# Early gathered rows taken out of their own phase and set among the scattered columns

## The chip, the cores and the metric

The kernel runs on one core of a Trainium2 chip. The metric is the device time of one execution in microseconds (us): the median of 3 runs of the kernel before is 1791.42 us (1790.85 to 1795.96). The profiled execution took 1794.13 us, of which the profile's span covers 1792.4 us. Engines are named as the profile names them: PE (matmul), PEld (its weight load), DVE (vector), ACT (scalar), POOL (GpSimd), SP (the queue that issues most DMAs).

## The reference

One decoder layer: an S5 branch and an mLSTM branch, merged by gates, and then a PEER expert mixer. Only the mixer is touched. For each of 512 tokens and 8 heads it finds the 16 best of 128 x 128 experts and adds up their value rows, weighted by a softmax gate and the expert's activation:

```python
q = (xb @ w_q).reshape(BLOCK, PEER_HEADS, 2, PEER_HALF)
s = jnp.einsum('thid,hikd->thik', q, keys32)
sv, si = lax.top_k(s, PEER_TOPK)                 # per half-key
cs, ci = lax.top_k(cand, PEER_TOPK)              # of the 16 x 16 sums
eidx = jnp.take_along_axis(cidx, ci, axis=-1)
gate = jax.nn.softmax(cs, axis=-1)
act = jax.nn.gelu(jnp.einsum('td,thkd->thk', xb, u_tab[eidx]))
return jnp.einsum('thk,thkd->td', gate * act, v_tab[eidx])
```

## The kernel before, in words

The 512 tokens are four tiles of 128. Tiles 1 to 3 are computed densely: for each of 128 blocks j of 128 experts, a hidden tile `h` = u_j x (the tokens of tiles 1 to 3) is made on PE in 24 matmuls of 128x384 (eight k steps of three matmuls, since each operand is split into a high and a low part: ACT makes `uh`, DVE makes `ul`), ACT applies the GELU (`act`), the result is multiplied by the dense gate (`w`), and products with v_j are added up in PSUM (`o`). Tile 0 is computed by gathering instead: for each of its 128 choices per token, POOL fetches one row per token of the table u (`fetch`, an indirect DMA of 512 KB) and DVE multiplies it with the tokens and adds up (`use`); later the same with rows of v.

The dense gates come by two ways. Tiles 2 and 3: `gates(i, ...)`, in 16 steps each of four one-hot instructions on DVE, 16 small matmuls on PE (`gp`), two evictions on ACT (`stg`), and a 2 MB store to DRAM (`gd`) after every fourth step. Tile 1: `scatter(n)`, which adds one column (one choice of each of the 128 tokens) into a zeroed array in DRAM (`gds`) by an indirect DMA with addition, issued by POOL. Columns of one head go beside each other; the first column of a head waits until all 16 columns of the head before have landed. Each is also put behind the last low split `wql` (`lows`), which POOL makes for the score blocks. The product phase reads `gds` only when the last head has landed.

What leads up to it: 16 score blocks (`scores(s_)`: the projection with w_q, the scores, the first top 16 on DVE); then `pairs_of` finds the 16 best pairs, per tile (tile 1 in two halves of four heads; the first half is traced in the middle of the score blocks, after block 8). The first half of tile 1's index list is `ix` (line 1170). `e0` (line 1293) is tile 0's index list, from which the gathers read.

The order of the work. `fill(us)` is called after each piece of that work with the piece's weight in us. It adds the weight to `done[0]`, issues two columns if columns have begun, and traces quarters of hidden tiles (two k steps) of the list `todo`, so that their count (280 quarters, 70 tiles) keeps step with `done[0]` over `whole` (236 us). Ten more tiles (`LEFT`) are traced behind all of that. The score loop issues two columns after each of the blocks 13 to 15 (line 1285). After the gates of tiles 2 and 3, `scatter(P)` issues what columns remain, and then `early()` asks for the first 40 (`NEARLY`) rows of u for tile 0, with four buffers, each used two fetches later, with `fill(1.3)` between. The buffers (`vraw`) are later those of the rows of v.

The trace order isn't yet the order on the engines: a planner orders the instructions of each engine ahead of the run, by trace order and by its own account of when operands are ready. `keep_in_program_order(i)` puts an instruction behind the instruction of the same engine that was traced just before it (it may be later, not earlier). On the chip each engine then takes its instructions in that fixed order. In the kernel before, the early gathers and their uses are pinned in this way and the columns are not.

Of the kernel before, what the change touches and what calls it, by code (L numbers as in the profile page):

```python
# [11 lines left out]
F32 = mybir.dt.float32  # L12
F32R = mybir.dt.float32r
BF16 = mybir.dt.bfloat16
# [9 lines left out]
P = 128  # L24
D = 1024
# [900 lines left out]
def peer(tc, a, out, dbg, cst, dram, xh, xl, blanks, ident, h2d, gds, x0, qt01, dump, split, mm3, rsqrt_cols):  # L926
# [21 lines left out]
    with es:  # L948
# [4 lines left out]
        ad = dram.tile([len(SP_), P, SD], F32, name="ad")  # L953
        acts = {}

        def load(j, eng):

            raw = up.tile([P, NK, P], F32, tag="uraw", name=f"u{j}", bufs=3)
            SY.dma_start(raw, a["ut"][j])
            hi = up.tile([P, NK, P], F32R, tag="uhi", name=f"uh{j}", bufs=3)  # L960
            lo = up.tile([P, NK, P], F32R, tag="ulo", name=f"ul{j}", bufs=3)
            split(hi, lo, raw, eng)
            return hi, lo

        def hidden(j, k0=0, k1=NK, eng=V):

            if k0 == 0:
                acts[j] = *load(j, eng), hps.tile([P, SD], F32, tag="h", name=f"h{j}")
            hi, lo, p = acts[j]
            for k in range(k0, k1):  # L970
                mm3(p, hi[:, k], lo[:, k], xh[k // 4][:, k % 4, P:], xl[k // 4][:, k % 4, P:], k == 0, k == NK - 1)
            if k1 == NK:
                acts[j] = up.tile([P, SD], F32, tag="act", name=f"act{j}", bufs=RA + 3)
                A.activation(acts[j], p, AF.Gelu_apprx_tanh)  # L974
                if j in SP_:
                    SY.dma_start(ad[SP_.index(j)], acts.pop(j))
# [13 lines left out]
        def fetch(s_, t):  # L990

            rows[s_], c = t, s_ % P
            return GP.indirect_dma_start(out=t, out_offset=None, in_=a["u"] if s_ < P else a["v"],  # L993
                                         in_offset=bass.IndirectOffsetOnAxis(ap=e0[:, c:c + 1], axis=0))

        def use(s_, jk):

            g, c = rows.pop(s_), s_ % P
            if s_ < P:
                i_ = V.scalar_tensor_tensor(jk, g, 1.0, x0, op0=OP.mult, op1=OP.mult, accum_out=hsl[:, c:c + 1])  # L1000
                if s_ == P - 1:
                    A.activation(hsl, hsl, AF.Gelu_apprx_tanh)
                    tt(w0, w0, hsl, OP.mult)
            elif c == 0:
                i_ = V.tensor_scalar(ac0, g, w0[:, 0:1], None, op0=OP.mult)
            else:
                i_ = V.scalar_tensor_tensor(ac0, g, w0[:, c:c + 1], ac0, op0=OP.mult, op1=OP.add)  # L1007
            return i_

        def early():  # L1010

            jk = rw.tile([P, D], BF16, name="jke", bufs=1)
            for n in range(NEARLY + 2):
                if n < NEARLY:
                    tc.keep_in_program_order(fetch(n, up.tile([P, D], F32, tag="vraw", name=f"ge{n}", bufs=4)))
                if n >= 2:
                    tc.keep_in_program_order(use(n - 2, jk))
                yield

        rp = ExitStack()  # L1020
        rm = rp.enter_context(tc.tile_pool(name="rm", bufs=1, reuse_waits="tile"))
# [151 lines left out]

        cols = []

        def scatter(n):

            for ix, wt, c in cols[:n]:
                i_ = GP.indirect_dma_start(out=gds.rearrange("b i j t -> (b i j t)").unsqueeze(1),  # L1179
                                           out_offset=bass.IndirectOffsetOnAxis(ap=ix[:, c:c + 1], axis=0),  # L1180
                                           in_=wt[:, c:c + 1], in_offset=None, compute_op=OP.add)

                h = c // TOPK
                if c % TOPK == 0:
                    heads.append([])
                for o in heads[h]:
                    tc.declare_no_dep(i_.ins, o.ins, reason="columns of one head")
                for o in heads[h - 1] if h else blanks:
                    behind(i_, o)
                heads[h].append(i_)  # L1190
                behind(i_, lows[-1])
            del cols[:n]

        heads = []
# [3 lines left out]
            tc.add_manual_dep(ins.ins, on.ins.name, mybir.DependencyInfo(  # L1198
                mybir.DependencyClass.Sync, mybir.DependencyReason.DATA), reason="gates added up")

        def gates(i, beside):

            ef, w = prs[i][1].rearrange("p h k -> p (h k)"), prs[i][2]
            p = mp.tile([P, 2, P], F32, tag="tr", name=f"et{i}")
            PE.transpose(p[:, 0], ef, ident)
            PE.transpose(p[:, 1], w, ident)
            ei = rw.tile([P, 2, P], I32, tag="ei", name=f"ei{i}", bufs=1)
            V.tensor_copy(ei[:, 0], p[:, 0])
            V.tensor_scalar(ei[:, 1], ei[:, 0], NKEY - 1, None, op0=OP.bitwise_and)
            V.tensor_scalar(ei[:, 0], ei[:, 0], 7, None, op0=OP.logical_shift_right)  # L1210
            eb = rw.tile([P, 2, P], F16, tag="eb", name=f"eb{i}", bufs=1)
            V.tensor_copy(eb, ei)

            wt = rw.tile([P, 2, P], F32, tag="wt", name=f"wt{i}", bufs=1)
            wb = rw.tile([P, 2, P], F16, tag="wb", name=f"wb{i}", bufs=1)
            V.tensor_scalar(wt[:, 0], p[:, 1], GS, None, op0=OP.mult)
            V.tensor_copy(wb[:, 0], wt[:, 0])
            tt(wt[:, 1], wt[:, 0], wb[:, 0], OP.subtract)
            V.tensor_copy(wb[:, 1], wt[:, 1])

            sh = [P, 4, P, 2]
            io_ = iob.unsqueeze(1).to_broadcast(sh)

            def each(x):
                return x.rearrange("p (a t) -> p a t", t=2).unsqueeze(2).to_broadcast(sh)
            for b in range(P // TB):
                stg = rw.tile([P, NKEY, TB], F32, tag="stg", name=f"stg{i}{b}")
                for q in range(TB // 8):
                    c = slice(b * TB + q * 8, b * TB + q * 8 + 8)
                    o1 = rw.tile(sh, F16, tag="o1", name=f"o1{i}{b}{q}")  # L1230
                    o2 = rw.tile(sh, F16, tag="o2", name=f"o2{i}{b}{q}")
                    ow = rw.tile([P, 2] + sh[1:], F16, tag="ow", name=f"ow{i}{b}{q}")
                    tt(o1, io_, each(eb[:, 0, c]), OP.is_equal)
                    tt(o2, io_, each(eb[:, 1, c]), OP.is_equal)
                    for n in range(2):
                        tt(ow[:, n], o2, each(wb[:, n, c]), OP.mult)
                    for h in range(2):
                        p = mp.tile([P, 4, P], F32, tag=("mm", "sc", "tr")[(2 * q + h) % 3], name=f"gp{i}{b}{q}{h}")
                        for t in range(4):
                            for n in range(2):  # L1240
                                a_, b_ = 2 * h + t // 2, t % 2
                                PE.matmul(p[:, t], o1[:, a_, :, b_], ow[:, n, a_, :, b_], start=n == 0, stop=n == 1)
                        t0 = 8 * q + 4 * h
                        A.activation(stg[:, :, t0:t0 + 4].rearrange("p j t -> p t j"), p, AF.Copy, scale=1.0 / GS)
                    fill(2.7)
                    for _ in range(2):
                        next(beside, None)
                SY.dma_start(gd[(i - 2) * (P // TB) + b], stg)

        def ready(j):  # L1250
# [6 lines left out]
        todo = [(j, h) for j in SP_[:-LEFT] for h in range(4)]  # L1257
        ntodo = len(todo)
        done = [0.0]

        whole = 4 * 24 + 2 * 16 * 2.75 + NEARLY * 1.3

        def fill(us):

            done[0] += us
            if heads:
                scatter(2)
            while todo and (ntodo - len(todo)) * whole < done[0] * ntodo:
                j, h = todo.pop(0)
                hidden(j, 2 * h, 2 * h + 2)  # L1270
# [6 lines left out]
        def beside_gates():  # L1277
            yield from filled(3)

        for s_ in range(NSEG):  # L1280
            scores(s_)
            if s_ == NSEG // 2:
                for _ in filled(1, 0, PH // 2):
                    pass
            if s_ > NSEG - 4:
                scatter(2)
        rq.close()
        rw = rp.enter_context(tc.tile_pool(name="rw", bufs=2, reuse_waits="tile"))
        for of in ((1, PH // 2, PH), (0,), (2,)):
            for _ in filled(*of):  # L1290
                pass
            if of == (0,):
                V.tensor_copy(e0, prs[0][1].rearrange("p h k -> p (h k)"))
        rest = beside_gates()
        for i in (2, 3):
            gates(i, rest)
        scatter(P)
        for _ in early():
            fill(1.3)
        for j, h in todo + [(j, h) for j in SP_[-LEFT:] for h in range(4)]:  # L1300
            hidden(j, 2 * h, 2 * h + 2)
        for j in range(RA):
            ready(j)
        rp.close()
# [150 lines left out]
```

## Time and profile before

| what | value |
|---|---|
| median of 3 runs | 1791.42 us (1790.85 to 1795.96) |
| profiled execution: time, span | 1794.13 us, 1792.4 us |
| PE busy | 1696.9 us (95% of the span) |
| DVE busy | 1314.6 us (73%) |
| ACT busy | 709.5 us (40%) |
| POOL busy | 728.7 us (41%) |
| mean granted TensorE clock | 0.978 |
| DMA | 412.11 MB, mean 230 GB/s |

How to read it: busy shares are means over the span, and stages differ. A wait is put down to what released it. A busy PE isn't PE at its peak, and spans on POOL are rough. A granted clock of 1.0 is 2.4 GHz, 0.5 is 1.2 GHz. In the timelines a row is: start in us, duration in us, engine, line, operation, output<-inputs, count, and in brackets the engine's idle time before it with what ended that. In tables of groups: busy us, mean ns of one | idle us before, with the releasers.

### The profile page before, as it was taken

The page shows a single profiled execution, that of the slowest core. Times are in us where ns is not written, and L with a number is a line of the kernel's source. Part 1 is how long each engine was busy: PE and PEld are TensorE (multiplying, and loading weights), DVE is VectorE, ACT ScalarE, POOL GpSimd, SP SyncE. Part 2 cuts the span into 40 slices and gives each one's busy share as a digit, 9 for nine tenths or more (in the row PEclk, how much of TensorE's full clock was granted, in tenths as well). Part 3 has the DMA queues.
Part 4 walks back from the last instruction along what each step waited for, and adds up shares of the span by engine and source line. Part 5 has one row for each costly group of instructions (what it writes and reads, how often), then busy time and mean ns, then how long its engine had stood idle before and what let it go on. Part 6 is the DMA issues. An engine that isn't in the chain of part 4 may idle for free. (4 is left out here: it accounts for less than half of the span.)

```text
span 1792.4 us, 25268 instructions
## 1 busy us (share of the span) xinstructions
PE 1696.9 (95%) x9196; PEld 1489.1 (83%) x9196; DVE 1314.6 (73%) x2584; ACT 709.5 (40%) x1064; POOL 728.7 (41%) x500
## 2 busy tenths in 40 slices
PE   5998989999999999999966999999999999999997
PEld 5988767776787889999956998888888888888885
DVE  7984583334657979996926668888878888888887
ACT  4533615443332324466732334333333333333333
POOL 2002433221313267787775433343333334444450
PEclk9989989999999999999987999999999999999999
DMA  4543325211343326768858999999899999999994
GB/s 164 126 77 91 105 95 176 71 48 36 120 178 137 113 52 167 178 201 258 245 159 310 360 378 383 348 328 376 326 356 327 363 324 363 323 363 322 334 340 177
DMA packets 206357, 412.11 MB, mean 230 GB/s; under 512 B 49176, under 2 KB 122904, under 8 KB 205080
## 3 DMA queue, kind: packets, MB, share of 16 engines
q1 hardware_dynamic: 142288, 267.49, 43.9%
q0 software_dynamic: 55296, 134.31, 22.6%
q10 hardware_dynamic: 8648, 8.70, 1.7%
q8 instruction: 72, 1.18, 0.3%
q14 instruction: 53, 0.43, 0.1%
HBM read 360.00 MB, written 47.28 MB: 227 GB/s over the span
## 5 line engine op out<-in xcount | busy, mean ns | idle before, releaser
L87 PE MATMUL h<-x2h,ul 128*128 128x384 f32 x1024 | 345.0, 337 | 31.0 <-DVE ul L80 31.0
L83 PE MATMUL h<-x2h,uh 128*128 128x384 f32 x1024 | 346.5, 338 | 3.0 <-ACT act L974 3.0
L86 PE MATMUL h<-x2l,uh 128*128 128x384 f32 x1024 | 344.7, 337 | 0.0
L86 PE MATMUL o<-vl,wh 128*128 128x512 f32 x768 | 299.7, 390 | 1.7 <-DVE vl L80 1.7
L87 PE MATMUL o<-vh,wl 128*128 128x512 f32 x768 | 295.3, 390 | 0.0
L83 PE MATMUL o<-vh,wh 128*128 128x512 f32 x768 | 286.8, 391 | 2.9 <-ACT wh L79 2.9
L993 POOL DMA_INDIRECT g<-in_v,e x128 | 168.6, 1317 | 238.0 <-DVE ac L1007 76.8
L1179 POOL DMA_INDIRECT gds<-gw,ix x128 | 235.4, 1839 | 61.1 <-issue 36.5
L87 PEld LDWEIGHTS h<-x2h,ul 128*128 128x128 f32 x1024 | 193.4, 189 | 33.3 <-DVE ul L80 31.3
L80 DVE TENSOR_TENSOR ul<-u,uh 128x1024 fp32r<-128x1024 f32 x128 | 156.1, 1220 | 87.6 <-ACT uh L79 82.9
L79 ACT ACTIVATE uh<-u 128x1024 fp32r<-128x1024 f32 x128 | 135.6, 1061 | 180.6 <-PE h L86 151.2
L83 PEld LDWEIGHTS h<-x2h,uh 128*128 128x128 f32 x1024 | 193.5, 189 | 5.8 <-ACT act L974 3.4
L86 PEld LDWEIGHTS h<-x2l,uh 128*128 128x128 f32 x1024 | 193.5, 189 | 2.5
L79 ACT ACTIVATE wh<-w 128x384 fp32r<-128x384 f32 x128 | 66.7, 524 | 296.8 <-issue 159.4
L993 POOL DMA_INDIRECT g<-in_u,e x88 | 111.8, 1271 | 175.7 <-DVE jk L1000 91.6
L80 DVE TENSOR_TENSOR vl<-v,vh 128x1024 fp32r<-128x1024 f32 x128 | 156.2, 1221 | 30.2 <-ACT vh L79 28.9
L83 PEld LDWEIGHTS o<-vh,wh 128*128 128x128 f32 x768 | 143.9, 188 | 33.1 <-ACT wh L79 4.9
L86 PEld LDWEIGHTS o<-vl,wh 128*128 128x128 f32 x768 | 144.2, 188 | 31.0 <-DVE vl L80 2.2
L87 PEld LDWEIGHTS o<-vh,wl 128*128 128x128 f32 x768 | 144.2, 188 | 29.0
L1007 DVE SCALAR_TENSOR_TENSOR ac<-g,w,ac 128x1024 f32<-128x1024 f32 x127 | 162.5, 1279 | 0.3
L79 ACT ACTIVATE vh<-v 128x1024 fp32r<-128x1024 f32 x128 | 134.0, 1049 | 62.8 <-PE o L87 56.8
L80 DVE TENSOR_TENSOR wl<-w,wh 128x384 fp32r<-128x384 f32 x128 | 70.5, 556 | 53.3 <-ACT wh L79 53.0
(540 smaller groups left out, 3170.8 us busy)
## 6 DMA issues: line engine op xcount, KB each, us to landing
u<-in_ut SPq DMA_DIRECT2D x128, 512.0 KB
v<-in_v SPq DMA_DIRECT2D x128, 512.0 KB
gd<-stg SPq DMA_DIRECT2D x8, 2048.0 KB
gi<-gd SPq DMA_DIRECT2D x32, 512.0 KB
ad<-act SPq DMA_DIRECT2D x80, 192.0 KB
acl<-ad SPq DMA_DIRECT2D x80, 192.0 KB
gds<-qt SPq DMA_DIRECT2D x8, 1024.0 KB
gi<-gds SPq DMA_DIRECT2D x32, 256.0 KB
```

Source lines behind the costliest of these rows:

```text
L79: A.activation(hi, src, AF.Copy)
L80: return eng.tensor_tensor(lo, src, f32(hi), op=OP.subtract)
L83: i_ = PE.matmul(ps, lh, rh, start=first, stop=False)
L86: PE.matmul(ps, lh, rl, start=False, stop=False)
L87: return PE.matmul(ps, ll, rh, start=False, stop=last)
L993: return GP.indirect_dma_start(out=t, out_offset=None, in_=a["u"] if s_ < P else a["v"], in_offset=bass.IndirectOffsetOnAxis(ap=e0[:, c:c ...
L1007: i_ = V.scalar_tensor_tensor(ac0, g, w0[:, c:c + 1], ac0, op0=OP.mult, op1=OP.add)
L1179: i_ = GP.indirect_dma_start(out=gds.rearrange("b i j t -> (b i j t)").unsqueeze(1), out_offset=bass.IndirectOffsetOnAxis(ap=ix[:, c:c + 1 ...
```

## The change

`early()` is removed. A list `clock[0]` counts PE's time in the order of tracing: 0.52 us for each k step of a hidden tile and 0.92 us for each gate step. A new function `beside()` is called in every `fill` from the end of the score blocks on (`paced[0]`), and after each quarter of the hidden tiles at the end. It reckons when POOL will be through with what was issued (`e["t"]`: 1.85 us a column, 4.5 us for the last of a head, 1.4 us a gather) and issues columns and gathers as long as that is not ahead of `clock[0]`. A gather comes in turn when columns beyond the 44th and gathers stand in the proportion 84 to 40. A row's use is placed when the count has passed its reckoned end by 12 us; it adds 1.3 to `done[0]`, as `early()` did through `fill`. No more than four rows (`NE`) are outstanding. Columns of this part are pinned in program order too. The score loop issues two columns after each of the blocks 9 to 15 instead of 13 to 15. `jke` is allocated when `e0` is written, in the same pool as before. The number of columns, gathers, uses and tiles stays the same.

```diff
+        clock = [0.0]
+            clock[0] += (k1 - k0) * 0.52          # in hidden()
-        def early():
...
+        NE = 4
+        FIRST = 44
+        early = dict(t=0.0, columns=0, got=[], used=0, jk=None)
+        def beside(flush=False):
+            e = early
+            while True:
+                t = 1e9 if flush else clock[0]
+                n = len(e["got"])
+                while e["used"] < n and e["got"][e["used"]] + 12.0 <= t:
+                    tc.keep_in_program_order(use(e["used"], e["jk"]))
+                    done[0] += 1.3
+                    e["used"] += 1
+                if e["t"] > t or not cols and n == NEARLY:
+                    break
+                if e["jk"] and n < NEARLY and (not cols or (e["columns"] - FIRST) * NEARLY > n * (P - FIRST)):
+                    if n - e["used"] == NE:
+                        break
+                    tc.keep_in_program_order(fetch(n, up.tile([P, D], F32, tag="vraw", name=f"ge{n}", bufs=NE)))
+                    e["t"] += 1.4
+                    e["got"].append(e["t"])
+                elif cols:
+                    scatter(1)
+                    e["t"] += 1.85 if e["columns"] % TOPK else 4.5
+                else:
+                    break
...
+            early["columns"] += len(cols[:n])     # in scatter()
+                if paced[0]:
+                    tc.keep_in_program_order(i_)
...
+                    clock[0] += 0.92              # in gates(), after each step
                     fill(2.7)
-                    for _ in range(2):
-                        next(beside, None)
+                    next(others, None)
+                    next(others, None)
...
+        paced = [False]
             done[0] += us                         # in fill()
-            if heads:
-                scatter(2)
+            if paced[0]:
+                beside()
...
-            if s_ > NSEG - 4:
+            if s_ > NSEG // 2:
                 scatter(2)
         rq.close()
+        paced[0] = True
             if of == (0,):
                 V.tensor_copy(e0, prs[0][1].rearrange("p h k -> p (h k)"))
+                early["jk"] = rw.tile([P, D], BF16, name="jke", bufs=1)
...
-        scatter(P)
-        for _ in early():
-            fill(1.3)
         for j, h in todo + [(j, h) for j in SP_[-LEFT:] for h in range(4)]:
             hidden(j, 2 * h, 2 * h + 2)
+            beside()
+        beside(True)
```

## Rows read from the trace of the kernel before

**Rows 1.** Windows: stretch, its us, busy (count) by engine; clock, DMA share, GB/s.

```profile
640.00:914.00 274.00, 274.00 (x1895) 265.06 (x1895) 237.09 (x724) 153.44 (x186) 217.20 (x116) 1.00 0.69 192
...
924.00:955.00 31.00, 0.27 (x1) 0.27 (x2) 5.16 (x8) 0.66 (x2) 23.07 (x18) 0.57 0.43 96
955.00:960.00 5.00, 5.00 (x19) 5.00 (x20) 5.00 (x7) 0.00 (x0) 3.80 (x3) 0.59 0.83 268
960.00:1058.00 98.00, 98.00 (x567) 98.00 (x566) 62.31 (x84) 34.01 (x48) 41.26 (x33) 1.00 0.99 367
1058.00:1072.00 14.00, 10.96 (x55) 10.64 (x54) 13.79 (x20) 6.10 (x9) 7.57 (x6) 0.88 1.01 377
1072.00:1300.00 228.00, 227.76 (x1070) 196.59 (x1069) 186.58 (x275) 82.42 (x111) 86.30 (x68) 1.00 0.98 353
```

**Rows 2.** Timeline of PE, the end and the new start around 924 to 955.

```profile
923.38 0.34 PE L86 MATMUL h<-x2l,uh 128*128 128x384 f32 x1
954.73 0.69 PE L87 MATMUL h<-x2h,ul 128*128 128x384 f32 x1 [31.01 <-DVE ul L80]
```

**Rows 3.** Timeline of DVE, 905 to 962.

```profile
911.33 1.23 DVE L80 TENSOR_TENSOR ul<-u,uh 128x1024 fp32r<-128x1024 f32 x1 [3.58 <-ACT uh L79]
947.65 1.23 DVE L1000 SCALAR_TENSOR_TENSOR jke<-ge,x 128x1024 bf16<-128x1024 f32 x1 [35.09 <-DMA ge<-in_u,e]
...
953.45 1.22 DVE L80 TENSOR_TENSOR ul<-u,uh 128x1024 fp32r<-128x1024 f32 x1
...
961.81 1.23 DVE L1000 SCALAR_TENSOR_TENSOR jke<-ge,x 128x1024 bf16<-128x1024 f32 x1 [1.43 <-DMA ge<-in_u,e]
```

**Rows 4.** Timeline of POOL, 641 to 944: columns (L1179), a split, the first gather.

```profile
641.34 1.78 POOL L1179 DMA_INDIRECT gds<-gw,ix  x1 [0.30 <-POOL wql L80]
...
651.99 2.41 POOL L80 TENSOR_TENSOR wql<-wq,wqh 128x1024 fp32r<-128x1024 f32 x1 [0.82 <-ACT wqh L79]
654.68 1.56 POOL L1179 DMA_INDIRECT gds<-gw,ix  x1 [0.28 <-POOL wql L80]
...
838.80 1.55 POOL L1179 DMA_INDIRECT gds<-gw,ix  x1 [6.91 <-DMA gds<-gw,ix]
...
939.78 1.56 POOL L1179 DMA_INDIRECT gds<-gw,ix  x1 [0.30 <-issue]
...
943.50 1.01 POOL L993 DMA_INDIRECT ge<-in_u,e  x1 [0.30 <-issue]
```

**Rows 5.** Groups of instructions by line, 600 to 1070.

```profile
L1179 POOL DMA_INDIRECT gds<-gw,ix x128 | 235.4, 1839 | 61.1 <-issue 36.5 <-DMA gds<-gw,ix 21.3 <-DVE m L945 2.5
...
L993 POOL DMA_INDIRECT ge<-in_u,e x40 | 51.7, 1293 | 62.5 <-DVE jke L1000 57.6 <-issue 3.7 <-DMA ge<-in_u,e 1.3
L1000 DVE SCALAR_TENSOR_TENSOR jke<-ge,x 128x1024 bf16<-128x1024 f32 x40 | 48.9, 1222 | 42.4 <-DMA ge<-in_u,e 42.0
...
L945 DVE TENSOR_TENSOR ow<-o,wb 128x1024 f16<-128x1024 f16 x64 | 41.1, 684 | 0.0
```

**Rows 6.** Line 1170, its two casts: ns min/median/max, first and last start.

```profile
L1170 DVE CAST ix<-ef x2: 175/185/195, 629.4 to 700.0; 128x64 int32<-128x64 f32 x2
```

**Rows 7.** Timeline of POOL, two early gathers.

```profile
949.15 0.94 POOL L993 DMA_INDIRECT ge<-in_u,e  x1 [0.88 <-DVE jke L1000]
...
953.81 1.68 POOL L993 DMA_INDIRECT ge<-in_u,e  x1 [1.29 <-DMA ge<-in_u,e]
```

**Rows 8.** Groups by line on POOL: first 912 to 943, then 800 to 912.

```profile
L1179 POOL DMA_INDIRECT gds<-gw,ix x16 | 24.9, 1557 | 7.2 <-issue 5.1 <-DMA gds<-gw,ix 2.1
...
L1179 POOL DMA_INDIRECT gds<-gw,ix x47 | 86.7, 1845 | 24.5 <-issue 13.7 <-DMA gds<-gw,ix 10.8
```

**Rows 9.** Windows of the matmuls on h alone: us, PE busy (count), clock, DMA.

```profile
0.00:669.00 669.00, 25.58 (x138) 0.97 0.35 106
669.00:777.00 108.00, 107.45 (x616) 1.00 0.68 171
...
960.00:1058.00 98.00, 98.00 (x567) 1.00 0.99 367
```

More of the change, by code (lines that the diff above doesn't have):

```diff
@@ L1008, in use @@
             return i_
-        def early():
[L1012 to L1018, printed above, removed]
         rp = ExitStack()
@@ L1199, in behind, with gates @@
                 mybir.DependencyClass.Sync, mybir.DependencyReason.DATA), reason="gates added up")
-        def gates(i, beside):
+        def gates(i, others):
             ef, w = prs[i][1].rearrange("p h k -> p (h k)"), prs[i][2]
```

## The prediction

> **What bounds the kernel now.** I began with the page's busy shares: PE works 95% of the span, so only a stretch in which PE stands still can give time back, and the window table finds it [rows 1]. From 640 to 914 us PE is busy without a gap, from 960 to 1058 again, and from 1072 on almost so; between 924 and 955 it works 0.27 of 31 us. The PE timeline gives the hole its ends [rows 2]: 31.01 us before the matmul at 954.73, which waits for DVE's `ul`. Behind the hole the granted clock is 0.59 for 5 us, PE's lower level, which loses another 0.41 x 5 = 2 us [rows 1]. PE is short once more around 1067: 3 us idle in 1058 to 1072, and about 1.5 us at the lower clock (0.88 in the mean) [rows 1].
>
> The DVE timeline says why [rows 3]. After the `ul` at 911.33 the next DVE instruction is the first early use (`jke`), and it waits 35.09 us for its gathered row. DVE takes its work in order, so the next `ul` comes at 953.45. The POOL timeline shows why that row is late [rows 4]: POOL sends scattered columns one behind another from 641.34 to 943.2, the last but one at 939.78, and the first gather stands behind them, at 943.50. From 641 to 943 POOL is the engine that is never free: the 128 columns cost 235.4 us busy and 61.1 us of gaps before them [rows 5], and two `wql` splits make up the rest of 302 us. So the hole is a late POOL, not a slow PE. The change puts 40 more instructions into that same queue.
>
> **The change part by part.** *Columns from block 9 instead of 13.* The first half of tile 1's index list is written at 629.4 [rows 6], so no column can go before that, however early it is traced. Between 629.9 and 654.7 POOL has 24.8 us; the four `wql` splits of about 2.4 us that fall there (one stands in the group) take some 11 us with their gaps [rows 4], and 13.8 us remain: 7 to 8 columns at 1.86 us. Before, 4 columns had gone by 654.68 [rows 4]. Gain: 4 columns, at 2.1 us some 8.5 us of POOL. Bounds: 0 (the planner leaves them where they were) and 11.7 (641.3 less 629.6).
>
> *Gathers in turn with columns.* Row n is asked for once (columns - 44) x 40 > 84 n: row 39 after 126 columns. POOL's order is then fixed, for each column and gather of the paced part is pinned behind the one before. In the kernel before, the 127th column starts at 939.78 [rows 4]. Hence row 39 is asked for at 939.8 - 8.5 + 39 gathers. What one costs there no row shows. The lower end is 0.94 + 0.30 = 1.24 us (a gather that met little of DVE, with its issue gap) [rows 7]; the upper is the mean of the 40 gathers beside `ul` and uses, 1.293 + 0.30 = 1.59 us [rows 5]. I take 1.59, since they move into a stretch where DVE is busier still: 237 of 274 us in 640 to 914, against 62 of 98 in 960 to 1058 [rows 1]. 39 x 1.59 = 62.0 us (lower end 48.4), so 993.3. Columns beside a busy DVE take 1.845 us in the mean, beside an idle one 1.557 [rows 8]; the last 14 before row 39 lose their idle DVE: + 4. Two gathers stand where a head's first column waits for the head before (columns 80 and 112), which hides 3.2 us. And in the stretch of my forecast DVE itself waits some 45 us, in which POOL sends about 21 instructions at the undisturbed price, 0.28 us less each: 6 us sooner. 993.3 + 4.1 - 3.2 - 6 = 988.2.
>
> The Trainium skill (SBUF — State Buffer, Who interferes with whom) has DVE and GpSimd share a port pair as an exclusive lock, in which the second to come is blocked for the whole instruction; it speaks against moving POOL's work beside DVE's. The trace bears out that DVE lengthens a column, by 0.29 us in the mean and not by a whole DVE instruction. If each gather met a whole 1.22 us use, that rule would make it 0.94 + 1.22 + 0.30 = 2.46 us, and the time 34 us more than by the row.
>
> From issue to the use's start the first row took 947.65 - 943.50 = 4.1 us with DMA nearly free, another 961.81 - 953.81 = 8.0 us with DMA full [rows 3, 4, 7]; I take 6 (the DMA share of 0.69 in 640 to 914 grows by the gathers' 20 MB). The last use can start at about **994**. The bounds, from gathers at 1.24 with the shorter landing and shorter head waits to head waits, landing and gathers all dearer, together 20 us, are 972 and 1014.
>
> *Uses at counted places.* Where does DVE come to the last use? Both counts follow from the code. Before: at use 0 the fills add up to 195.6 (106.6 for the pairs, 86.4 for the 32 gate steps, 2.6), so 233 quarters of a hidden tile were traced, 242.3 us at 1.04, and with 32 gate steps of 0.92 the count is 271.8. PE ran dry at 923.7 [rows 2], so it runs dry 651.9 us past the count of a use that blocks DVE. That a hidden tile of 24 matmuls takes about 4.16 us shows in 960 to 1058: 98.0 us for 567 of them [rows 9]. After: a use is placed when the count passes POOL's reckoned time plus 12. For row 39 that is 105 columns x 1.85 + 7 x 4.5 + 40 x 1.4 + 12 = 293.8; the next step has 297.6 (25 gate steps and 264 quarters). So PE runs dry at 651.9 + 297.6 = **949.5** if row 39 isn't there. The reckoning gives 112 columns and 40 gathers 281.8 us; the rows give 112 x 2.36 (302 over 128) + 63.6 = 328. The margin of 12 is smaller than that gap.
>
> PE starts again a use (1.22 + 0.08) and an `ul` (1.22) later [rows 3, 5], at 996.5. PE idle: 996.5 - 949.5 = **47 us**, spread over the uses from about the tenth on, against 31 us. This is the stall's new place: the same DVE queue, behind a gather that is late because POOL is still the bound. All of that queue stands behind it: `ul`, the gate steps' one-hots, and through them PE and ACT.
>
> *What costs nothing.* The 40 uses (1.30 us, 52 us in all [rows 5]) and the hidden tiles that come forward with them load DVE by about 1.30 + 2.6 + 1.25 x 1.22 = 5.4 us per gate step of 6.1 us (four one-hot instructions of 0.64 make the 2.6 [rows 5]); that fits, barely, under PE. If it didn't, PE would wait some 0.5 us at each of 32 steps. `jke` moves at no cost. SP issues no DMA more; loads of u come sooner, in step with the tiles. After the last use some 60 us of hidden tiles run without gathers, so v rows and gates are there early: the 4.5 us around 1067 go away.
>
> *Sum.* PE lost 31.0 + 2.0 + 4.5 = 37.5 us; it will lose 47. Small stalls at a full clock cost nothing more. Change: +9.5 us. From the profiled execution of 1794.1 us (span 1792.4) that is 1803.6; from the median of 1791.4, which the forecast is about, **1801**.
>
> **Rivals.** *A, POOL stays the bound* (above): 1801, range 1779 to 1821 by the bounds 972 and 1014 for the last use (PE idle 25 to 67). For it: POOL has no idle between 641 and 943 but issue gaps and head waits [rows 4, 5]. Against it: none of the columns' prices was measured beside uses.
>
> *B, the uses meet their rows* (the other side). The planner may leave a use later than its pin when its own account has the row late, putting `ul` of later tiles ahead of it; then DVE never stands and PE has hidden tiles to fill the time. It decides from the point at which some eleven tiles (45 us at 4.16) go ahead of the last use. For it: by 777 PE had run 25.6 + 107.5 = 133 us of hidden tiles, where the traced order has 101 before the first gate step [rows 9]. Against: in the kernel before, the planner set use 0 right at its pin although the row was 35 us off [rows 3], so its POOL is faster than the real one. PE then loses 0 to 18 us: 1754 to 1772, middle 1760.
>
> *C, dearer still.* The gathers' 512 KB go through the same DMA engines as u, `ad` and the 2 MB gate stores, with a share of 0.69 before 914 and 0.99 where the gathers run [rows 1]. If a head's first column then waits 8 us instead of about 4 (6.91 was seen [rows 4]) and each POOL instruction meets more of DVE, the last use comes 20 to 35 us later than in A: 1821 to 1836. By the Trainium skill's lock (SBUF — State Buffer, Who interferes with whom) the time would lie there too.
>
> *D, nothing moves*: the gather phase only trades places, the loss of 47 shrinks to 37: within 5 us of 1791.
>
> **How the numbers follow.** A measurement of this kernel tells about 0.3%, 5.4 us, from no change. A has 0.53 (0.09 faster, 0.13 same, 0.31 slower), B 0.27, C 0.15, D 0.05. Faster 0.36, same 0.18, slower 0.46. The forecast is A's 1801. Since both signs hold much of the chance, A's own range is 1779 to 1821, and the range that should hold 8 in 10 reaches into B and C: 1758 to 1822.
>
> **What would show it.** Right: the POOL timeline alternates columns and gathers until about 985 to 995 without idle other than issue gaps and head waits; DVE's uses wait for `ge` from about the tenth on, 40 us or more in sum; PE's idle from 780 to 1000 is small pieces that add up to about 47 us, before `ul`; nothing is idle near 1067. Wrong: the uses wait under 20 us in sum (B, the time then near 1760); or the first column before 629 or a gather mean under 1.3 us with its gap; or DMA at 1.0 and head waits of 8 us (C). A clock that drops at the many small stalls would add to A.

## Result, and the profile after

The changed kernel takes 1814.13 us (median of 4 runs, 1812.99 to 1817.57) against 1791.13 us for the kernel before beside it: a ratio of 1.0128, 95% interval 1.0103 to 1.0153. It is slower, as forecast, and inside the range, but by 23.0 us where the forecast said 9.5. In the profiled execution the span grows from 1792.4 to 1815.8 us. PE works 9196 matmuls in both; its busy time goes from 1696.9 to 1706.2 us and its idle time, span less busy, from 95.5 to 109.6.

The window table of the changed kernel has the columns of [rows 1]. Where the kernel before had one hole, there are six short stretches now, and from 1000 to 1080 us PE lacks nothing:

```profile
640.00:760.00 120.00, 117.17 (x649) 112.15 (x648) 101.27 (x486) 44.68 (x59) 97.55 (x51) 0.99 0.54 132
760.00:800.00 40.00, 26.74 (x161) 25.82 (x160) 28.62 (x73) 10.87 (x14) 33.90 (x21) 0.83 0.74 212
800.00:840.00 40.00, 31.52 (x202) 30.40 (x201) 28.52 (x50) 17.55 (x22) 30.24 (x18) 0.87 0.76 217
840.00:880.00 40.00, 40.00 (x265) 38.74 (x264) 31.67 (x47) 20.01 (x25) 30.81 (x19) 1.00 0.90 276
880.00:920.00 40.00, 30.81 (x206) 28.60 (x204) 20.77 (x30) 17.37 (x21) 29.74 (x20) 0.91 0.81 245
920.00:960.00 40.00, 33.91 (x228) 32.54 (x229) 30.80 (x49) 15.69 (x20) 28.86 (x18) 0.91 0.85 236
960.00:1000.00 40.00, 26.45 (x189) 24.89 (x188) 24.23 (x37) 17.32 (x21) 31.18 (x19) 0.83 0.80 245
1000.00:1040.00 40.00, 40.00 (x324) 38.49 (x324) 34.09 (x50) 27.93 (x33) 8.95 (x6) 1.00 0.91 330
1040.00:1080.00 40.00, 40.00 (x243) 39.75 (x242) 19.11 (x21) 17.46 (x24) 9.31 (x8) 1.00 0.96 360
```

The PE idle of these rows adds up to 53.4 us, against some 34 us in the hole and around 1067 before [rows 1, 2]. PE's timeline gives the stops (the four longest are shown); it shows what the engine waited for in brackets:

```profile
775.85 0.69 PE L87 MATMUL h<-x2h,ul 128*128 128x384 f32 x1 [12.85 <-DVE ul L80]
...
834.72 0.69 PE L87 MATMUL h<-x2h,ul 128*128 128x384 f32 x1 [8.48 <-DVE ul L80]
...
924.38 0.69 PE L87 MATMUL h<-x2h,ul 128*128 128x384 f32 x1 [7.20 <-DVE ul L80]
...
991.61 0.37 PE L1268 MATMUL gp<-ow,o 128*128 128x128 f16 x2 [13.43 <-DVE ow L945]
```

It is the releaser of [rows 2], `ul`, or another output of DVE. DVE's timeline has the early uses, the answer to [rows 3]; six of them wait long, the others little or not at all:

```profile
769.84 1.23 DVE L1003 SCALAR_TENSOR_TENSOR jke<-ge,x 128x1024 bf16<-128x1024 f32 x1 [16.82 <-DMA ge<-in_u,e]
...
830.44 1.23 DVE L1003 SCALAR_TENSOR_TENSOR jke<-ge,x 128x1024 bf16<-128x1024 f32 x1 [11.48 <-DMA ge<-in_u,e]
...
882.53 1.23 DVE L1003 SCALAR_TENSOR_TENSOR jke<-ge,x 128x1024 bf16<-128x1024 f32 x1 [10.02 <-DMA ge<-in_u,e]
...
921.31 1.23 DVE L1003 SCALAR_TENSOR_TENSOR jke<-ge,x 128x1024 bf16<-128x1024 f32 x1 [10.07 <-DMA ge<-in_u,e]
...
942.81 1.23 DVE L1003 SCALAR_TENSOR_TENSOR jke<-ge,x 128x1024 bf16<-128x1024 f32 x1 [6.70 <-DMA ge<-in_u,e]
...
989.12 1.22 DVE L1003 SCALAR_TENSOR_TENSOR jke<-ge,x 128x1024 bf16<-128x1024 f32 x1 [12.19 <-DMA ge<-in_u,e]
```

In sum the 40 uses waited 82.3 us, in 16 of them. POOL's timeline, the answer to [rows 4], says why the waits are few and long (L1203 is a column, L996 a gather):

```profile
752.33 1.79 POOL L1203 DMA_INDIRECT gds<-gw,ix  x1 [3.58 <-DMA gds<-gw,ix]
...
765.58 1.00 POOL L996 DMA_INDIRECT ge<-in_u,e  x1 [0.30 <-issue]
...
806.93 1.55 POOL L1203 DMA_INDIRECT gds<-gw,ix  x1 [4.58 <-DMA gds<-gw,ix]
...
824.48 1.54 POOL L1203 DMA_INDIRECT gds<-gw,ix  x1 [0.30 <-issue]
826.32 1.00 POOL L996 DMA_INDIRECT ge<-in_u,e  x1 [0.30 <-DMA gds<-gw,ix]
827.62 1.56 POOL L1203 DMA_INDIRECT gds<-gw,ix  x1 [0.30 <-issue]
829.49 0.98 POOL L996 DMA_INDIRECT ge<-in_u,e  x1 [0.30 <-issue]
830.78 2.33 POOL L1203 DMA_INDIRECT gds<-gw,ix  x1 [0.30 <-issue]
833.41 0.99 POOL L996 DMA_INDIRECT ge<-in_u,e  x1 [0.30 <-issue]
```

From 806.93 to 824.48 nine columns run without a gather, and then gathers and columns alternate one to one. Each later head of 16 columns has such a block too, of seven to nine columns. The first gather of the kernel goes at 765.58 behind 55 columns, where the code asks for it behind 48: its proportion would have it behind 45, but `jke`, which it needs, is allocated only then. So the first row behind each block is late by the block, and its use, which has its place by the count, holds DVE. The first line shows one thing more: column 48 starts at 752.33, and in the kernel before it started at 752.35, although the columns now begin earlier.

The groups by line, the answer to [rows 5], leave the prices as they were:

```profile
L1203 POOL DMA_INDIRECT gds<-gw,ix x128 | 238.3, 1862 | 70.4 <-issue 34.1 <-DMA gds<-gw,ix 32.4 <-PE q L86 2.2
L996 POOL DMA_INDIRECT ge<-in_u,e x40 | 51.0, 1275 | 12.2 <-issue 8.2 <-DVE jke L1003 0.9 <-DVE o L945 0.9
```

### The profile page after: what moved, and what is told of

Same layout as the page of the kernel before. It is cut to its first block, busy times and chain, and to the rows that moved or that the text cites. A ratio compares the mean times of both kernels' runs of the same rounds, so it can differ in the third digit from the quotient of the medians.

```text
span 1815.8 us, 25263 instructions
## 1 busy us (share of the span) xinstructions
PE 1706.2 (94%) x9196; PEld 1495.6 (82%) x9196; DVE 1313.3 (72%) x2584; ACT 709.0 (39%) x1064; POOL 753.5 (41%) x500
## 4 chain that ended last, share of the span: by engine, by line
PE 64%; POOL 10%; DVE 7%; DMA 6%; issue 5%; ACT 1%; ACTq 0%; POOLq 0%; DVEq 0%
PE o L86 9%; PE o L87 9%; PE o L83 9%; POOL gds L1203 8%; PE h L83 5%; PE h L86 5%; PE h L87 5%; DMA gds<-gw,ix 3%; PE q L87 1%; PE q L86 1%; PE q L83 1%; PE n L814 1%; POOL ge L996 1%; PE s L804 1%; DMA ge<-in_u,e 1%
## 5 line engine op out<-in xcount | busy, mean ns | idle before, releaser
L83 PE MATMUL o<-vh,wh 128*128 128x512 f32 x768 | 296.9, 389 | 0.0
L996 POOL DMA_INDIRECT g<-in_v,e x128 | 172.6, 1349 | 233.0 <-PE o L87 161.9
L1203 POOL DMA_INDIRECT gds<-gw,ix x128 | 238.3, 1862 | 70.4 <-issue 34.1
L996 POOL DMA_INDIRECT g<-in_u,e x88 | 131.0, 1489 | 216.6 <-PE o L87 159.4
L1003 DVE SCALAR_TENSOR_TENSOR jk<-g,x 128x1024 bf16<-128x1024 f32 x88 | 107.4, 1221 | 46.0 <-PE o L87 40.3
```

What stands on the lines that cost most here:

```text
L83: i_ = PE.matmul(ps, lh, rh, start=first, stop=False)
```

## Experiments

Theory Q: a use stands in DVE's order at a point which POOL's queue hasn't reached, so what counts is POOL's order, the count and POOL's load. Its rivals: O, only the blocks of columns do it; L, DVE has too much to do in the stretch; M, the gathers' transfers make the tiles of u late. Each ratio is to runs of the kernel before on the same chip; PE's idle is each profile's span less PE's busy time. e5_half leaves out part of the work and serves as a test alone.

| kernel | us | ratio to before, 95% | PE idle | PE busy |
|---|---|---|---|---|
| before | 1791.13 | | 95.5 | 1696.9 |
| changed | 1814.13 | 1.0128 [1.0103, 1.0153] | 109.6 | 1706.2 |
| e1_order | 1806.63 | 1.0076 [1.0048, 1.0104] | 97.9 | 1709.0 |
| e2_count | 1787.38 | 0.9956 [0.9937, 0.9976] | 79.0 | 1708.2 |
| e3_both | 1781.46 | 0.9931 [0.9915, 0.9948] | 77.8 | 1703.0 |
| e4_cols | 1790.46 | 0.9983 [0.9958, 1.0009] | 87.1 | 1700.5 |
| e5_half | 1752.78 | 0.9773 [0.9757, 0.9790] | 58.7 | 1690.7 |
| e6_cols13 | 1816.71 | 1.0129 [1.0112, 1.0146] | 109.7 | 1705.0 |
| e7_late | 1776.38 | 0.9893 [0.9871, 0.9915] | 75.3 | 1701.9 |
| e8_tail | 1783.21 | 0.9937 [0.9915, 0.9959] | 84.1 | 1698.4 |
| e9_rows24 | 1782.05 | 0.9933 [0.9909, 0.9957] | 73.7 | 1703.0 |
| e10_before24 | 1790.12 | 0.9984 [0.9970, 0.9999] | 88.1 | 1703.6 |
| e11_later_use | 1791.21 | 0.9995 [0.9977, 1.0012] | 91.7 | 1697.0 |
| e12_later_use_cols | 1794.33 | 1.0013 [0.9996, 1.0030] | 94.4 | 1697.5 |

### e1_order: the exact turn

```
+        def turn(ins, behind_these):
+            for o in behind_these:
+                tc.add_manual_dep(ins.ins, o.ins.name, ...NoSync...)
-                    tc.keep_in_program_order(i_)          # a column
+                    turn(i_, fetched[-1:])
+                    between.append(i_)
-                    tc.keep_in_program_order(fetch(n, ...))
+                    f_ = fetch(n, ...)
+                    turn(f_, between or fetched[-1:])
```

> The changed kernel, but each column of the paced part is put behind the last gather traced and each gather behind all columns traced since the one before. In the trace of the changed kernel nine or ten columns of each head run in one block ahead of its gathers; here two columns and a gather take turns through the head. Theory Q (uses stand in DVE's queue at a place that POOL's queue hasn't reached): rows early in a head come some 15 us sooner, the last ones as before, so PE's loss between 640 and 1040 falls from about 65 us (53 idle, 10 to 12 at a low clock) to about 50 to 58, spread over more and shorter stalls: 1799 to 1808 us. Theory O (the blocks alone are to blame, in turn the rows would be on time): under 20 us of PE's loss, 1755 to 1772. Theory L (DVE is overloaded by 40 uses beside the gate steps) and theory M (the gathers' bytes make u late): nothing changes, 1810 to 1818.

The blocks are gone; POOL sends two columns, a gather, two columns, to the end. Rows 38 and 39 on POOL's timeline:

```profile
989.43 2.02 POOL L996 DMA_INDIRECT ge<-in_u,e  x1 [0.30 <-DMA ad<-act]
991.75 2.08 POOL L1212 DMA_INDIRECT gds<-gw,ix  x1 [0.30 <-issue]
994.13 1.55 POOL L1212 DMA_INDIRECT gds<-gw,ix  x1 [0.30 <-issue]
995.99 1.00 POOL L996 DMA_INDIRECT ge<-in_u,e  x1 [0.30 <-issue]
```

and the last two uses on DVE's:

```profile
1002.76 1.23 DVE L1003 SCALAR_TENSOR_TENSOR jke<-ge,x 128x1024 bf16<-128x1024 f32 x1 [8.63 <-DMA ge<-in_u,e]
...
1007.45 1.22 DVE L1003 SCALAR_TENSOR_TENSOR jke<-ge,x 128x1024 bf16<-128x1024 f32 x1
```

1806.63 us, as Q expected: the blocks cost some 8 us (1814.13 to 1806.63; the intervals of the two ratios just touch). The uses still wait, 71.4 us in 21 places, so theory O is not enough.

### e2_count: a slower count, the blocks left

```
-        early = dict(t=0.0, ...
+        early = dict(t=15.0, ...
-                    e["t"] += 1.4
+                    e["t"] += 1.6
-                    e["t"] += 1.85 if e["columns"] % TOPK else 4.5
+                    e["t"] += 2.15 if e["columns"] % TOPK else 6.5
```

> The changed kernel, with POOL's time counted as the trace of it shows: 2.15 us a column, 6.5 us for the last of a head, 1.6 us a gather, the count begun at 15 us instead of 0. The same instructions; uses come later in DVE's queue, by up to some 65 us. Theory Q: the uses meet their rows, PE's loss in this phase falls from 65 us to 0 to 15: 1754 to 1770 us. Theory L: DVE has the same work in the same stretch plus the tail, PE still loses 30 us or more: 1785 to 1815. Theory M: u is late wherever the gathers run, 1785 to 1815, with PE waiting for ul behind uh behind DMA and not behind a use.

1787.38 us: 27 us less than the changed kernel with blocks still there, the same work and the same transfers. So the places that the count gives the uses cost that much. But it is 17 us above what Q expected, and within the 1785 to 1815 of L and M. PE still idles 23.6 us between 640 and 1080, so this run alone doesn't refute them; e5_half does.

### e3_both: both edits

> Both edits: columns and gathers strictly in turn, and POOL's time counted as the trace shows. Theory Q: as with the slower count alone or a little better, 1754 to 1766 us. Theory O: as with the order alone. Theories L and M: 1785 to 1815.

1781.46 us, faster than both kernels, but 15 us above the expectation. The trace shows where the count is still too fast: POOL needed 85 us from the first gather (743.21) to the eleventh (828.43), while the count gives 70 for the 21 columns and 10 gathers between (the expectation of e7_late says 68). Two columns of that stretch on POOL's timeline, and a use at its end on DVE's:

```profile
769.22 6.73 POOL L1212 DMA_INDIRECT gds<-gw,ix  x1 [0.30 <-issue]
776.26 6.82 POOL L1212 DMA_INDIRECT gds<-gw,ix  x1 [0.31 <-issue]
```

```profile
843.78 1.22 DVE L1003 SCALAR_TENSOR_TENSOR jke<-ge,x 128x1024 bf16<-128x1024 f32 x1 [5.43 <-DMA ge<-in_u,e]
```

The two columns stand beside a DVE that works 38.98 of the 40 us from 760 to 800.

### e4_cols: the kernel before with the early columns alone

```
-            if s_ > NSEG - 4:
+            if s_ > NSEG // 2:
```

> The kernel before, with one part of the change alone: two columns after each of the score blocks 9 to 15 instead of 13 to 15. POOL's first column goes at 630 instead of 641. Theory Q: the hole of 31 us before the first use shrinks by what POOL's last column comes sooner, 8.5 us as predicted, or 0 if the columns beside the pairs take longer in turn, as the changed kernel's trace has it at column 48 (752.33 against 752.35): 1782 to 1792 us. Rival: the columns between the w_q splits hold up the score blocks, PE loses 3 to 10 us there: 1794 to 1801.

The hole shrinks from 31.0 [rows 2] to 22.6 us and PE starts 6.6 us sooner (948.09 against 954.73). But 3.0 us of these were there before any column went: this execution writes the index list at 626.32, the kernel before at 629.37 [rows 6]. Little arrives: 0.9983, which can't be told from no change. A new stop of 2.8 us before `q` waits for a `wql` split of POOL, which is the rival's loss in small, and the stop around 1067 is 4.1 us instead of 3.0.

### e5_half: POOL's load taken away

```
             for ix, wt, c in cols[:n]:
+                if c % 2 and c > 15:
+                    continue
```

> The changed kernel, but from column 16 on every second scattered column isn't sent (56 of 128 are left out, so part of tile 1's gates is missing from the output); the counts, the places of the uses, the gathers, the uses and the hidden tiles stay. POOL loses some 56 x 2.15 = 120 us of work before row 39; DVE's work and the gathers' bytes are the same. Theory Q (uses stand where POOL's queue has not arrived): the uses wait under 10 us in sum instead of 82, PE idles at most some 6 us between 640 and 1080, and the time falls to 1750-1762. Theory L (DVE has too much to do in this stretch): DVE's work is unchanged, so the stalls stay, at least 1795. Theory M (the gathers' transfers make the tiles of u late): the gathers are unchanged, at least 1795.

1752.78 us, and PE stops for under 4 us in all. Its waits from 600 to 1300 (us, times, longest), and what DVE sat idle for ahead of the early uses (us, times):

```profile
PE q L87 <- POOL wql L80: 2.8, 1, 2.8
PE h L87 <- DVE ul L80: 0.8, 1, 0.8
```

```profile
  DMA ge<-in_u,e: 12.9, 7
```

DVE has the same uses, the gathers the same bytes (DMA share 0.89 to 1.01 from 800 to 960), and gathers and columns still alternate one to one. L and M fall: the loss is POOL's load against the places of the uses. The blocks of columns are gone here as well; by e1_order they are some 8 of the 61 us.

### e6_cols13: the changed kernel without the early start

The line of e4_cols, undone in the changed kernel.

> The changed kernel with its columns beginning after block 13 again, as before the change. By the prediction's step (4 columns gained, 8.5 us of POOL at every later row) the rows come 8.5 us later and each long stall grows: about 1822. By the trace of the changed kernel, in which column 48 starts at the same time as before (752.33 against 752.35), nothing is left of the early start when the first gather goes: 1810-1818, no difference that can be measured.

1816.71 us, 1.0129 against 1.0128: no difference that can be measured. But this doesn't price POOL's time alone. The last gather does go later, at 1015.19 instead of 1005.07. And the places of the uses move with it: the count now holds eight more columns, and by the code the use of row 39 stands at 308.6 instead of 297.6. The row and its use both come some 10 us later.

### e7_late: another 8 us of margin

```
-        early = dict(t=15.0, ...       # e3_both
+        early = dict(t=23.0, ...
```

> The kernel of e3_both (exact turn, slower count) with the count set back another 8 us (it starts at 23 instead of 15). In e3_both POOL needed 85 us from the first gather to the eleventh where the count gave 68, and the uses between 835 and 890 waited 3 to 5 us each. Theory Q: these waits go, PE's 6 us stop at 856 too; but POOL still sends its last gather at about 1019, and the uses left over at the end hold up the lows of the next tiles to about 1026, so part is given back there: 1770-1778. If the stalls left in e3_both were DVE's load (L) or the transfers (M), eight us of margin change nothing: 1779-1784.

1776.38 us, as Q expected, and the least of the kernels that do all the work: 0.9893 of the kernel before, 38 us under the changed one. What PE still lost is small at the uses, and one stop at the end:

```profile
848.08 0.44 PE L87 MATMUL h<-x2h,ul 128*128 128x384 f32 x1 [2.95 <-DVE ul L80]
...
1039.67 0.69 PE L83 MATMUL h<-x2h,uh 128*128 128x384 f32 x1 [9.53 <-ACT act L977]
```

### e8_tail: work for PE ahead of the last uses

```
-        beside(True)
         for j in range(RA):
             ready(j)
+            beside()
+        beside(True)
```

with the count started at 27.

> The kernel of e3_both with the count set back 12 us (start 27), and the six tiles that are made ready for the products placed ahead of the last left-over uses instead of behind them, which gives PE up to 25 us of work while POOL sends its last rows. Theory Q: both the waits at 835-890 and the stop at the end go: 1760-1770, the best so far. Theories L and M: 1779-1786, as e3_both or worse, since DVE and DMA have the same work in the same stretch.

1783.21 us: a miss, and inside the range of L and M. But PE's stops before `ul` come to 3.0 us in sum; what grew is the stop at the end, to 19.87 us, although the six tiles now stand ahead of the last uses. POOL's last column, then loads that SP sends behind it, then what DVE waits for, each from its engine's timeline:

```profile
1024.19 1.55 POOL L1212 DMA_INDIRECT gds<-gw,ix  x1 [0.30 <-issue]
```

```profile
1027.19 0.38 SPq L1368 DMA_DIRECT2D gi<-gds  x1
...
1032.56 0.41 SPq L1290 DMA_DIRECT2D acl<-ad  x1
```

```profile
1047.02 0.56 DVE L945 TENSOR_TENSOR w<-gi,acl 128x384 f32<-128x384 f32 x1 [18.19 <-DMA acl<-ad]
```

The load of the summed gates waits for all 128 columns, and it stands in SP's queue ahead of loads of v and of `acl`, which leave only after 1027.19. So POOL holds the products through the last column. The loads of v also need the buffers of the last rows, whose uses end at 1026.5; no run separates the two.

### e9_rows24: fewer early rows

```
-    NEARLY = 40
+    NEARLY = 24
```

in e7_late.

> The kernel of e7_late with 24 early rows instead of 40; the 16 others are gathered and used among the products, with the 88 that were there. In e7_late PE stood 9.5 us at 1039.67 because the load of the summed gates waits for POOL's last column, at 1022.47. Theory Q (POOL's queue sets both the rows and that load): 16 gathers x 1.58 = 25 us less ahead of the last column, so it goes near 998, the stop at 1039 and its low clock (2 us) go and the waits at 840-880 get shorter: 1758-1768. If instead the products have no room for 16 more gathers and uses, or the stop has another cause, the time stays at 1774-1784.

1782.05 us: a miss again. The last column does go early (976.34), and the stops at the end are gone but for 2.2 us in sum. (Fewer rows free the buffers of v sooner, too.) But a stop of 6.44 us appears at 789.44, and the 16 rows put off are missing at the end: the last matmul is at 1760.00 and the span 1776.7, so 16.7 us lie behind its start instead of 11.6 in e7_late (1765.57 and 1777.2). The spans are alike although this execution began 5.5 us ahead: it writes the index list at 624.63, e7_late at 630.17.

### e10_before24: the same in the kernel before

> The kernel before the change with 24 early rows instead of 40, all behind the 128 columns as before: the control for e9_rows24. The hole hangs on the first gather, which stands behind the same columns, so by theory Q it stays near 31 us, and the time is 1787-1795, no difference that can be measured. If fewer early rows were by themselves what helps, it would be under 1780; if the products lose by 16 more rows, over 1797.

1790.12 us: the time stays, but not for the reason given: the hole didn't stay at 31 us. With fewer uses in the total, more of the hidden tiles were handed out ahead of the first use, and the stops at `ul` add up to 12.7 us. Of the 18 us that the hole lost some 12 reappear behind the last matmul, 23.4 us (1768.25 to 1791.7) instead of 11.6 before, and 6.7 in PE's busy time. That asked for the next pair.

### e11_later_use and e12_later_use_cols: the hole filled, nothing else

```
-        whole = 4 * 24 + 2 * 16 * 2.75 + NEARLY * 1.3
+        whole = 4 * 24 + 2 * 16 * 2.75 + 24 * 1.3
```

in the kernel before (e11), and the line of e4_cols as well (e12).

> The kernel before the change with one number altered: the share of tile work that is handed out counts 24 early uses instead of 40, so that some 22 quarters of a hidden tile more (22 x 1.04 = 23 us of PE) are traced ahead of the first early use; POOL's queue, the 40 rows and their order stay. Theory Q, by which the hole is the time that DVE reaches a use ahead of its row: PE runs dry some 21 to 23 us later while the row comes when it came, so the hole shrinks from 31 to 8-10 us and the time is about 1771. Rival (the 40 rows are landed only by 1060 whatever is traced where, so the work put ahead of the hole is missing behind it): PE stands idle near 1035-1065 for what the hole lost, 1785-1793.

> The kernel of e11_later_use with the columns beginning after block 9, which in e4_cols took the hole from 31 to 22.6 us. Theory Q: 31 - 8.4 - 22 leaves no hole, PE is busy from 640 on but for some 3 us for a split on POOL, and the time is 1760-1768. Rival as above (work is missing behind the hole instead): 1782-1792.

1791.21 and 1794.33 us: no change, and the rival held. In e11 PE's timeline has its three longest stops, and DVE's the first use, the last one and what follows it:

```profile
951.69 0.69 PE L87 MATMUL h<-x2h,ul 128*128 128x384 f32 x1 [8.85 <-DVE ul L80]
...
965.69 0.45 PE L87 MATMUL h<-x2h,ul 128*128 128x384 f32 x1 [3.19 <-DVE ul L80]
...
1065.40 1.65 PE L83 MATMUL o<-vh,wh 128*128 128x512 f32 x3 [19.15 <-ACT wh L79]
```

```profile
949.27 1.23 DVE L1000 SCALAR_TENSOR_TENSOR jke<-ge,x 128x1024 bf16<-128x1024 f32 x1 [19.05 <-DMA ge<-in_u,e]
...
1062.76 1.23 DVE L1000 SCALAR_TENSOR_TENSOR jke<-ge,x 128x1024 bf16<-128x1024 f32 x1 [2.16 <-DMA ge<-in_u,e]
...
1063.91 0.55 DVE L945 TENSOR_TENSOR w<-gi,acl 128x384 f32<-128x384 f32 x1
```

The hole is 8.85 and 3.19 us instead of 31.0, and 19.15 us are lost at the first product, whose `w` stands behind the fortieth use in DVE's order. In the kernel before the fortieth row is asked for at 1056.5 and used at 1065.1; in e11 the two times are 1056.57 and 1062.76. In e12 the stops are 10.75, 2.39 and 21.72 us.

## Why the prediction was right in its side and wrong in its size

**What bounds the kernel: right, with one reading missing.** POOL's queue is the bound, through the uses in DVE's order; e5_half shows it, and neither DVE's load nor the transfers. What the prediction took as the loss, the hole, is only where PE's spare time fell: e11_later_use emptied most of it and gained nothing, because the fortieth row ends the stage. By this reading a changed order of the rows pays through an earlier last use and not through a filled hole: it comes at 1023.6 in e7_late instead of 1065.1. The changed kernel has it at 1012.6, but PE stood 53.4 us up to there. No run moves the last use alone, so this stays a reading of the traces.

**The order of POOL: the step that failed.** "POOL's order is then fixed, for each column and gather of the paced part is pinned behind the one before": the trace shows blocks of seven to nine columns instead. In the code the columns of one head are declared free of each other, and the blocks lie within heads; with the turn written out as dependencies they vanish (e1_order). That the declaration undoes the pins is the likely reason; the declaration alone wasn't taken away. Of the 13 us by which the time is above the forecast, e1_order, which has the order as assumed, gives some 8 to the blocks; the other 5 to 6 are the prices, below. In the trace the row that decides is not row 39 but row 34, the first behind the last block. The count of its use is 272.0 by the code, so by the prediction's own rule PE runs dry at 651.9 + 272.0 = 923.9, and it starts again at 991.61: 67.7 us, some at the lower clock, where the forecast had 47. That is 20.7 us more, blocks and prices together, and 9.5 + 20.7 = 30.2, while the spans differ by 23.4. Of the 6.8 us between, 4.3 come back behind 1080 us, where PE idles 11.7 us instead of 16.0, for which the forecast had no term; the rest stays open.

**The prices: right for the gather, wrong for the early columns and the landing.** With the order as assumed, e1_order takes 1806.6 us where the forecast was 1801. There row 39 was asked for at 995.99, not 988.2. A gather cost 1.275 + 0.305 = 1.58 us in the changed kernel, as taken (1.59). The lock of the Trainium skill (SBUF — State Buffer, Who interferes with whom), which the prediction weighed at 2.46 us a gather, isn't borne out as a price here. The Trainium skill ties the block for a whole instruction to DVE's 2-port modes there, a condition that the prediction left out; no run here shows the mode of the uses. What was missing are the 8.5 us of the early columns, against the kernel before: column 31 of the changed kernel still starts 5.9 us sooner (703.80 against 709.65), column 40 no longer does (731.31 against 730.83), and one between took 4.38 us. The landing was too short as well: row 38 was used 13.3 us after its issue (989.43 to 1002.76), where 6 was taken. Both together are more than the 5.6 us; e1_order has the 4.3 us behind 1080 too.

**What was not costed.** Columns moved ahead of POOL's `wql` splits delay a split: PE stops 2.8 us for it in the changed kernel and in e1 to e5, e7 and e8, 1.7 us in e9 and e12, and not in e6_cols13, which has no early start. The last score matmul of the changed kernel starts 46.3 us behind the index list (629.54 to 675.85), before the change 39.6 (629.37 to 668.94); 2 us of this are matmuls on `h` that went ahead of it. The prediction counted those splits as POOL's time only.

**Small stalls.** "Spread over the uses from about the tenth on" and small: wrong. The first use waits 16.82 us, and six stops carry the loss. They cost clock too: PE's busy time for the same matmuls grew by 9.3 us, and 57 of the matmuls on `h` between 640 and 1080 ran at the lower of the two levels, against 22 before. That isn't a loss on top of the 67.7 us, since the late row sets when PE goes on.

**The rivals.** B, the uses meet their rows, didn't come about here, but it is what e7_late approaches with a count that is 23 us later and slower per instruction. C's signs are there in part: a head's first column waited up to 9.29 us, and from 840 to 880 DMA's share was 0.90. That nothing is idle near 1067 held.

## What to carry to other kernels

An order that the program asks for is a wish until the trace shows it: read the engine's timeline, and write the turn out as dependencies where it matters (8 us here). An instruction that waits for another queue belongs behind the measured pace of that queue under load, with margin; too early on an in-order engine it stops all that stands behind it (27 us here for a few numbers in the count). And a hole in the bounding engine isn't a loss by itself: first find what ends the stage, since filling the hole (e11_later_use) moved most of its microseconds to the stage's end.

## What the runs showed of the hardware

**A column's price.** A scattered column takes 1.56 us on POOL beside an idle DVE [rows 8], and in e3_both two took 6.73 and 6.82 us beside a DVE at 0.97. DVE's share doesn't settle it: in the kernel before DVE works all 40 us from 760 to 800, and there the columns took 1.7 to 2.5 us and one took 9.38:

```profile
785.95 2.04 POOL L1179 DMA_INDIRECT gds<-gw,ix  x1 [0.30 <-issue]
790.45 9.38 POOL L1179 DMA_INDIRECT gds<-gw,ix  x1 [2.46 <-DVE m L945]
```

DVE ran TENSOR_TENSOR instructions of the same kinds beside the short ones and the long one. What tells them apart stays open; one price per instruction doesn't describe it.

**PE's clock behind a stop.** The stop of 12.85 us in the changed kernel was followed by 5.0 us at the lower of PE's two levels, 1.2 GHz (a matmul on `h` every 0.32 us, then every 0.174 us):

```profile
775.85:780.81 4.96, 4.96 (x15) 4.96 (x16) 4.96 (x17) 0.00 (x0) 4.04 (x4) 0.50 0.82 248
780.81:785.00 4.19, 4.19 (x26) 4.15 (x26) 3.61 (x9) 1.44 (x2) 3.58 (x3) 1.00 1.02 321
```

So this stop cost some 2.3 us more than its idle time. A stop of 2.95 us at 848.08 in e7_late had no slow matmul behind it, and one of 3.14 us at 877.28 there had nine; what tells them apart stays open.
